# Half of the Winograd weight sums and most left factors made ahead and kept in DRAM, with 35 seven-product quads instead of 26, in an fp32 attention + SSM layer

## The chip, the cores and the metric

One core of a Trainium2 chip runs the kernel. The metric is the device time of one execution in microseconds, as the median of several runs. The engines named below are TensorE (PE, matmuls, with its weight loads shown as PEld), VectorE (DVE), ScalarE (ACT), GpSimd (POOL) and SyncE (SP), whose queue issues nearly all DMAs.

## The reference, cut to what matters

One layer on 256 rows of 2048 values, all in float32. A wide projection feeds an attention half (16 heads of 128) and a state-space half (SSM: 8 groups, 64 heads of 64, state 128, chunks of 128); two sigmoid gates weigh their branches.

```python
hn = rms_norm(x, norm_w)
proj = hn @ w_in            # q, k, v, z_a, z_s, xbc, dt, g_a, g_s
...                         # o_a: attention, times silu(z_a)
...                         # y: conv + SSD scan, times silu(z_s), rms_norm
merged = sigmoid(g_a) * (o_a @ w_attn_branch) + sigmoid(g_s) * (y @ w_ssm_branch)
x = x + merged @ w_out      # then a last rms_norm
```

## The kernel before, in words

**Weights.** The host packs all weights (`lay_weights`, L107) into `wall`, 480 units of 128 x 1024 float32 (512 KB each), in the order in which `weight_plan` (L56) lists the products. A unit passes through one pipeline. `load` (L207) issues its DMA on SP's queue into one of `W_BUFS` = 4 buffers with the tag "w". `unit` (L213) has ACT copy it, rounded, into h (L222) and DVE compute the rest l = w - h (L223), each into one of `H_BUFS` = 4 buffers. The activations are split in the same way, so XT holds high and low halves side by side, and a float32 product becomes h·xh + h·xl + l·xh on PE. The h and l instructions are issued at a priority raised by `L_AHEAD` = 120.

**Stages, in order of time** (by the profile):
- up to 33 us: the first four blocks and dt.
- 33 to 594 us: the SSM part (L759). Each of 8 groups projects B, C and four pairs xs, zs with `gemm_a` (L256, two units each): a "group" of ten projections, 60.1 us where no gate stands in it. Three of the `gs` gate blocks run before groups 0 and 4 and one after group 7 (`gates` L469 with `gemm_b` L330, eight units each). Around these come `conv` (L623), `make_cb` (L634: a product cbp on PE, then cb on DVE), `decays` (L640: ACT, and gt on DVE), `turn` (L661: eight transposes on PE, xdt on DVE), and `scan` (L679: yp on PE, L687; then y, ssq and the split of y into yT on DVE and ACT).
- 594 to 875 us: products of two 512-column blocks with `gemm_pair` (L369): `ssm` blocks 0 and 2 (y times w_ssm_branch, called w_ssm below), then `v` 0 and 2 and `ga` 2.
- 875 to 1175 us: attention (L905). Each of 16 heads projects q, k and za; `scores` (L863: sps on PE, then the softmax on DVE and ACT), `turn_p` (L886: three transposes ptp on PE) and `mix` (L892: ops on PE, then za and oaT on DVE) of earlier heads stand between them.
- up to 1393 us: gates `ga` 0 and 1, the pair `attn` 0, `attn` 2 and 3 by `gemm_b`, the pairs `out` 0 and 2, and the last norm.

**Pairs and quads.** `gemm_pair` works on two row tiles by two column blocks. A quad is two contraction tiles (q counts them), so 2x2 blocks times 2x2 blocks: 8 block products of three matmuls, 24 matmuls. For the quads listed in `S_QUADS` (L40) it uses the Strassen-Winograd form with seven products, 21 matmuls. This form needs four sums of weight blocks: t13 (L432, two of them in one instruction) and two more (L437, L438), all on DVE, each sum then split into h and l (L425, L426). It needs sums of activation blocks too, the "left factors" sx: `turn_x` (L348 to L366), one 512-column addition, four of 128 columns and the splits. Each left factor is made once just ahead of the pair that uses it first (L820 for y, L842 for x, L903 in `mix` for the attention output, sxt_o, and L968) and stays in SBUF for the second pair. `fold` (L458) adds the seven products together.

**Order.** `after`, `tick` and `run_due` (L239 to L254) are a due list written out by hand: a call of `after(n, f)` has f emitted n ticks later, and each projection or quad is one tick (a gate block four). Y_LAG, CB_LAG, GT_LAG, TURN_LAG and S_LAG (L36) are such lags. From the emitted program, Tile's scheduler fixes one order of instructions for each engine when the program is built; at run time each engine works through its own order and waits on semaphores.

Of the kernel before, what the change touches and what calls it, by code (L numbers as in the profile page):

```python
# [9 lines left out]
F32 = mybir.dt.float32  # L10
F32R = mybir.dt.float32r
# [4 lines left out]
P = 128  # L16
S = 256
# [89 lines left out]
def lay_weights(mats):  # L107
    out = np.empty((N_UNITS, P, UNIT), np.float32)
    for tag, form, src, off, n_kt, w in PLAN:
# [6 lines left out]
        if form == "p":  # L116
# [3 lines left out]
            for q in range(n // 2):  # L120
                f = FIRST[tag] + 2 * q
                if q in S_QUADS[tag]:
                    out[f] = np.concatenate([m[q, 0, :, 0], m[q, 1, :, 1]], axis=1)
                    out[f + 1] = np.concatenate([m[q, 0, :, 1], m[q, 1, :, 0]], axis=1)
                else:
                    out[f : f + 2] = m[q].reshape(2, P, UNIT)
# [46 lines left out]
def hybrid_block(ctx: ExitStack, tc: tile.TileContext, wall, xt, x, pk_d, cst_d, fw_d, out):  # L173
# [31 lines left out]
    on_unit = {}  # L205

# [22 lines left out]
    def split(src, hi, lo, scale=1.0):  # L229
# [3 lines left out]
        else:  # L233
            ve.scalar_tensor_tensor(lo, src, scale, hi.bitcast(F32), ALU.mult, ALU.subtract)

# [112 lines left out]
    def turn_x(pool, bufs, temp, x, spare=0):  # L348


        sx = pool.tile([P, 2, 4 - spare, P], F32R, name=f"sx{now[0]}", tag="sx", bufs=bufs)
# [9 lines left out]
        parts = [(sx[:, 0, n], sx[:, 1, n]) for n in range(4 - spare)]  # L361
        if spare:
            own = x[:, 0, P:S], x[:, 0, S + P :]
            split(s[:, 0], *own)
            parts.insert(0, own)
        split(s[:, spare:], sx[:, 0], sx[:, 1])  # L366
        return parts

    def gemm_pair(tag, x_of, n_kt, sxs, swap, extra={}, close=1):  # L369
# [20 lines left out]
        for q in range(n_q):  # L390
            tick()
            if q in extra:
                extra[q]()
# [20 lines left out]
            for m in (n, n + 1):  # L414
                if m not in loaded:
                    load(m)
            wa, wb = loaded.pop(n), loaded.pop(n + 1)
# [11 lines left out]
            with tc.high_priority(L_AHEAD):  # L429
                t13 = mul.tile([P, UNIT], F32, name=f"t13_{n}", tag="t13", bufs=1)  # L430
                b12 = wb[:, :512].unsqueeze(1).to_broadcast([P, 2, 512])
                ve.tensor_tensor(two(t13), b12, two(wa), ALU.subtract)  # L432
# [3 lines left out]
                part(wb[:, 512:], hc[:, :512], lc[:, :512])  # L436
                ve.tensor_tensor(wb[:, :512], wa[:, 512:], t13[:, :512], ALU.subtract)  # L437
# [8 lines left out]
            for acc, x, h, l, cs, own in (  # L446
                (prods[0], a[0][0], ha, la, lo, True),
                (es[1], sx[3], ha, la, hi, False),
                (es[0], a[0][1], hc, lc, lo, False),
                (prods[1], sx[0], ht, lt, lo, True),  # L450
                (prods[3], sx[1], ht, lt, hi, True),
                (prods[2], sx[2], hu, lu, lo, True),
# [101 lines left out]
    with tc.tile_pool(name="ssm", bufs=2) as sp:  # L554
# [203 lines left out]

        for g in range(GROUPS):  # L759
# [9 lines left out]
            for t in range(max(4 * g, 1), 4 * g + 4):  # L769
# [4 lines left out]
                if t % 4 == 3:  # L774
# [6 lines left out]
                    after(y_lag, lambda a=(g, state): scan(*a), 1)  # L781
                conv(collect(acc, f"x{t}"), t, state["xs"][-1][:, i], f"x{t}")
# [25 lines left out]
    def blocks(t, c):  # L808
        return [t[:, i, (c + j) * 512 : (c + j + 1) * 512] for i in range(2) for j in range(2)]

    def two_kts(t, q):
        return t[:, 2 * q : 2 * q + 2, :]

    with tc.tile_pool(name="xp", bufs=1) as xp:
        sxs = {}
        for c in (0, 2):
            for q in S_QUADS[("ssm", c)]:
                if q not in sxs:
                    temp = xp.tile([P, 4, 512], F32, name=f"sxt_y{q}", tag="tmp", bufs=1)
                    sxs[q] = turn_x(xp, 6, temp, two_kts(yT[q // 8], q % 8), 1)  # L820
            es, prods = gemm_pair(
                ("ssm", c), lambda kt: yT[kt // 16][:, kt % 16, :], 2 * KT, sxs, c == 2,
# [210 lines left out]
```

## Time and profile before

| | before |
|---|---|
| median of 3 runs | 1395.88 us (1394.46 to 1396.6) |
| profiled execution: span | 1392.9 us |
| what the median of the runs has above that span | 3.0 us |
| PE, DVE, ACT, POOL busy | 99%, 78%, 58%, 2% |
| DMA over the span | 272.33 MB, 196 GB/s mean |
| w loads | 480 of 512 KB, 3.8 us from issue to landing (median) |

The profiled execution has no time of its own beside its span; what the runs have above it is what lies around the program. The page's second part cuts the span in 40 equal slices:

```
PE   9999999999999999999999999999999999999997
DVE  6897887776787787798988988766676666487887
ACT  7656676675667586665554555555554544454454
DMA  8766675756566665656666566655555655667564
```

Each digit is the busy share of a slice of 34.8 us in tenths (9 is 90% or more). The groups of instructions by line give engine, output and inputs, count, then busy time, mean ns of one, and the idle time just ahead of them with what ended most of it. A busy time of PE counts from start to modelled end, and consecutive matmuls overlap.

### The profile page before, as it was taken

The numbers are of one execution on the slowest core, as the hardware profiler recorded it, in microseconds if no ns is written. First come the engines' busy times: TensorE is split into PE (matmuls) and PEld (weight loads), VectorE is DVE, ScalarE is ACT, GpSimd is POOL, SyncE is SP. The second block draws the span as 40 slices with busy tenths as digits, with TensorE's granted clock in tenths as the row PEclk, the third lists the DMA queues.
The fourth block names the chain that finished last, engine by engine and source line by source line (L and its number), as shares of the span: only waits on it lengthen the run. The fifth ranks groups of instructions, "written<-read, shape, count | busy, mean of one in ns | idle before, by whom it ended". The sixth has DMA issues, their size and how long they took to land.

```text
span 1392.9 us, 19889 instructions
## 1 busy us (share of the span) xinstructions
PE 1381.8 (99%) x7308; PEld 1176.8 (84%) x7308; DVE 1086.8 (78%) x1622; ACT 811.5 (58%) x1258; POOL 32.1 (2%) x86
## 2 busy tenths in 40 slices
PE   9999999999999999999999999999999999999997
PEld 7888888888888888888888888888888888888885
DVE  6897887776787787798988988766676666487887
ACT  7656676675667586665554555554554544454454
POOL 1300000000000000000000000000000000000010
PEclk9999999999999999999999999999999999999999
DMA  8766675756566665656666566655555655667564
GB/s 328 243 196 185 197 215 163 221 185 204 172 212 174 208 189 180 194 181 211 192 206 202 187 212 191 217 174 174 168 174 174 181 170 176 199 212 250 172 198 136
DMA packets 78210, 272.33 MB, mean 196 GB/s; under 512 B 8800, under 2 KB 9376, under 8 KB 77728
## 3 DMA queue, kind: packets, MB, share of 16 engines
q1 hardware_dynamic: 77392, 269.88, 61.9%
q8 instruction: 57, 0.93, 0.3%
q10 hardware_dynamic: 720, 1.18, 0.2%
q14 instruction: 41, 0.34, 0.1%
HBM read 268.86 MB, written 2.16 MB: 195 GB/s over the span
## 4 chain that ended last, share of the span: by engine, by line
PE 98%; DVE 1%; DMA 0%; issue 0%; ACT 0%; SPq 0%; POOL 0%; POOLq 0%; DVEq 0%
PE ps_zs L265 8%; PE ps_xs L265 8%; PE ps_zs L268 4%; PE ps_za L265 4%; PE ps_k L265 4%; PE ps_q L265 4%; PE ps_xs L268 4%; PE ps_ssm L384 3%; PE ps_ssm L385 3%; PE ps_ssm L386 3%; PE ps_q L268 2%; PE ps_k L268 2%; PE ps_za L268 2%; PE ps_gs L345 2%; PE ps_gs L343 2%; PE ps_gs L344 2%
## 5 line engine op out<-in xcount | busy, mean ns | idle before, releaser
L223 DVE TENSOR_TENSOR l<-w,h 128x1024 fp32r<-128x1024 f32 (+1 forms) x432 | 522.8, 1213 | 231.0 <-ACT h L222 229.3
L222 ACT ACTIVATE h<-w 128x1024 fp32r<-128x1024 f32 (+1 forms) x432 | 452.8, 1051 | 407.6 <-issue 104.5
L265 PE MATMUL ps_zs<-XT,h 128*128 128x512 f32 x496 | 174.6, 394 | 0.0
L265 PE MATMUL ps_xs<-XT,h 128*128 128x512 f32 x496 | 174.0, 393 | 0.0
L268 PE MATMUL ps_zs<-XT,l 128*128 128x256 f32 x496 | 139.2, 281 | 0.0
L268 PE MATMUL ps_xs<-XT,l 128*128 128x256 f32 x496 | 138.9, 280 | 0.0
L265 PEld LDWEIGHTS ps_zs<-XT,h 128*128 128x128 f32 x496 | 93.0, 187 | 21.3
L265 PEld LDWEIGHTS ps_xs<-XT,h 128*128 128x128 f32 x496 | 92.9, 187 | 20.9
L268 PEld LDWEIGHTS ps_zs<-XT,l 128*128 128x128 f32 x496 | 93.5, 188 | 1.2 <-issue 1.2
L268 PEld LDWEIGHTS ps_xs<-XT,l 128*128 128x128 f32 x496 | 93.5, 189 | 0.0
L265 PE MATMUL ps_q<-XT,h 128*128 128x512 f32 x256 | 92.3, 404 | 0.0
L265 PE MATMUL ps_k<-XT,h 128*128 128x512 f32 x256 | 89.8, 395 | 0.0
L265 PE MATMUL ps_za<-XT,h 128*128 128x512 f32 x256 | 89.7, 394 | 0.0
L268 PE MATMUL ps_q<-XT,l 128*128 128x256 f32 x256 | 71.1, 278 | 0.0
L268 PE MATMUL ps_za<-XT,l 128*128 128x256 f32 x256 | 71.0, 278 | 0.0
L268 PE MATMUL ps_k<-XT,l 128*128 128x256 f32 x256 | 71.0, 277 | 0.0
L385 PE MATMUL ps_ssm<-l,yT 128*128 128x512 f32 x168 | 65.3, 390 | 0.0
L386 PE MATMUL ps_ssm<-h,yT 128*128 128x512 f32 x168 | 65.0, 389 | 0.0
L384 PE MATMUL ps_ssm<-h,yT 128*128 128x512 f32 x168 | 57.5, 390 | 0.0
L265 PEld LDWEIGHTS ps_za<-XT,h 128*128 128x128 f32 x256 | 48.0, 188 | 11.3
L265 PEld LDWEIGHTS ps_k<-XT,h 128*128 128x128 f32 x256 | 48.0, 188 | 11.2
L265 PEld LDWEIGHTS ps_q<-XT,h 128*128 128x128 f32 x256 | 48.1, 188 | 10.9
(520 smaller groups left out, 2984.3 us busy)
## 6 DMA issues: line engine op xcount, KB each, us to landing
w<-in_wall SPq DMA_DIRECT2D x480, 512.0 KB, 3.8
acb<-acum_d SPq DMA_DIRECT2D x32, 256.0 KB, 3.6
th_s<-in_x SPq DMA_DIRECT2D x4, 512.0 KB, 6.5
vth<-in_x SPq DMA_DIRECT2D x1, 2048.0 KB, 9.3
early<-in_xt SPq DMA_DIRECT2D x7, 256.0 KB, 6.9
fw<-in_fw SPq DMA_DIRECT2D x1, 1024.0 KB, 5.5
out<-vth SPq DMA_DIRECT2D x4, 256.0 KB, 2.8
out<-vth ACTq DMA_DIRECT2D x4, 256.0 KB, 3.2
```

The lines of the kernel that those rows point to most:

```text
L222: ac.activation(h[:, a:b], w[:, a:b], AF.Copy)
L223: ve.tensor_tensor(l[:, a:b], w[:, a:b], h[:, a:b].bitcast(F32), ALU.subtract)
L265: pe.matmul(acc, h[:, kk, :], m, start=(kt == 0), stop=False)
L268: pe.matmul(acc[:, S:], l[:, kk, :], m[:, :S], start=False, stop=(kt == KT - 1))
L343: pe.matmul(accs[i], xh, h[:, kk], start=(kt == 0), stop=False)
L344: pe.matmul(accs[i], xh, l[:, kk], start=False, stop=False)
L345: pe.matmul(accs[i], xl, h[:, kk], start=False, stop=(kt == KT - 1))
L384: pe.matmul(acc, xh, h, start=start, stop=False)
L385: pe.matmul(acc, xh, l, start=False, stop=False)
L386: pe.matmul(acc, xl, h, start=False, stop=stop)
```

## The change

`S_QUADS` lists 35 quads instead of 26: `ssm` 0 and 2 have eight each (five and six before), `v` 0 three (two before), `v` 2, `ga` 2 and `attn` 0 four each (three before); `out` 0 and 2 keep their two each.

**Weight sums.** For each of the 35 quads, a new function `sum_weights` runs ahead of time: it loads one unit (t) and half of another (tb) into two buffers of the "w" ring, and one tick later DVE subtracts twice (512 columns each), and a tick after that `spill` stores the result, 512 KB, from the buffer to a DRAM tile on SP's queue. 27 of these stand in the SSM part, one per 2.5 ticks from tick 16 on (SUMS_SSM); eight, for `attn` and `out`, stand in attention, one per 4 ticks from tick 6 on (SUMS_ATT). `lay_weights` lays the two units of such a quad out the other way to match.

**Left factors.** `keep_left` makes the four of x and the eight of y during the SSM part, with their temporary in the "w" ring and the result in the "h" ring, and stores them (512 KB for one of x, 384 KB for one of y). `fetch_left` loads them at the pair stages: the y factors three quads ahead of their use, the x factors at the start of the `v` pairs. Those of the attention output are made in `mix` as before, but with the temporary in the "w" ring.

**The quad.** A seven-product quad loads unit n (wa), the kept sum (wt) and half of unit n + 1 (wc), three buffers of the ring instead of two; DVE has one subtraction of 1024 columns left (instead of one of 1024 and two of 512), and four splits as before, in another order. `t13` is gone.

```diff
 S_QUADS = {
-    ("ssm", 0): (5, 7, 9, 11, 13), ("ssm", 2): (3, 5, 7, 9, 11, 13),
-    ("v", 0): (4, 6), ("v", 2): (2, 4, 6), ("ga", 2): (2, 4, 6),
-    ("attn", 0): (2, 4, 6), ("out", 0): (3, 5), ("out", 2): (3, 5),
+    ("ssm", 0): (2, 4, 5, 7, 8, 10, 11, 13), ("ssm", 2): (2, 4, 5, 7, 8, 10, 11, 13),
+    ("v", 0): (2, 4, 6), ("v", 2): (2, 4, 5, 6), ("ga", 2): (2, 4, 5, 6),
+    ("attn", 0): (2, 4, 5, 6), ("out", 0): (3, 5), ("out", 2): (3, 5),
 }
+SX_Y = S_QUADS[("ssm", 0)]
+SX_X = S_QUADS[("v", 2)]
+SUMS_SSM = [(t, q) for t in (("ssm", 0), ("ssm", 2), ("v", 0), ("v", 2), ("ga", 2)) for q in S_QUADS[t]]
+SUMS_ATT = [(t, q) for t in (("attn", 0), ("out", 0), ("out", 2)) for q in S_QUADS[t]]
+SSM_FROM, SSM_EVERY, ATT_FROM, ATT_EVERY = 16, 2.5, 6, 4
...
+    presum, lefts = {}, {}
+    def ring(name):
+        return stream.tile([P, UNIT], F32, name=name, tag="w", bufs=W_BUFS)
+    def spill(kept, key, name, src, n):
+        kept[key] = dram.tile([P, n], F32, name=name, tag=name)
+        nc.sync.dma_start(kept[key], src)
+    def sum_weights(tag, q):
+        n = FIRST[tag] + 2 * q
+        t, b11 = ring(f"t{n}"), ring(f"tb{n}")
+        nc.sync.dma_start(t, wall[n + 1])
+        nc.sync.dma_start(b11[:, :512], wall[n, :, :512])
+        def add():
+            ve.tensor_tensor(t[:, :512], t[:, :512], b11[:, :512], ALU.subtract)
+            ve.tensor_tensor(t[:, 512:], t[:, 512:], t[:, :512], ALU.subtract)
+        after(1, add)
+        after(2, lambda: spill(presum, (tag, q), f"t_{tag[0]}{tag[1]}_{q}", t, UNIT))
...
+    def keep_left(key, x, spare):
+        name = f"{key[0]}{key[1]}"
+        temp = ring(f"sxt_{name}").rearrange("p (n m) -> p n m", n=2)
+        sx = stream.tile([P, UNIT], F32R, name=f"sx_{name}", tag="h", bufs=H_BUFS)
+        n = 2 * (4 - spare) * P
+        turn_x(sx[:, :n].rearrange("p (e n s) -> p e n s", e=2, n=4 - spare), temp, x, spare)
+        after(1, lambda: spill(lefts, key, f"sxd_{name}", sx[:, :n].bitcast(F32), n))
...
+    def fetch_left(pool, bufs, key, x, spare):
+        sx = new_sx(pool, bufs, spare, f"{key[0]}{key[1]}")
+        nc.sync.dma_start(sx.bitcast(F32), lefts[key].rearrange("p (e n s) -> p e n s", e=2, n=4 - spare))
+        return left_parts(sx, x, spare)
...
-            wa, wb = loaded.pop(n), loaded.pop(n + 1)
+            wa, wt, wc = ring(f"w{n}"), ring(f"wt{n}"), ring(f"wc{n}")
+            nc.sync.dma_start(wa, wall[n])
+            nc.sync.dma_start(wt, presum[tag, q])
+            nc.sync.dma_start(wc[:, :512], wall[n + 1, :, 512:])
...
-                t13 = mul.tile([P, UNIT], F32, name=f"t13_{n}", tag="t13", bufs=1)
-                b12 = wb[:, :512].unsqueeze(1).to_broadcast([P, 2, 512])
-                ve.tensor_tensor(two(t13), b12, two(wa), ALU.subtract)
                 ha, la = hl(stream, "a", "hl", H_BUFS)
                 part(wa, ha, la)
                 hc, lc = hl(stream, "c", "hl", H_BUFS)
-                part(wb[:, 512:], hc[:, :512], lc[:, :512])
-                ve.tensor_tensor(wb[:, :512], wa[:, 512:], t13[:, :512], ALU.subtract)
-                ve.tensor_tensor(wb[:, 512:], wb[:, 512:], wb[:, :512], ALU.subtract)
+                part(wc[:, :512], hc[:, :512], lc[:, :512])
+                t2 = wt[:, 512:].unsqueeze(1).to_broadcast([P, 2, 512])
+                ve.tensor_tensor(two(wa), two(wa), t2, ALU.subtract)
                 ht, lt = hl(mul, "t", ("ht", "lt"), 2)
-                part(t13, ht, lt)
+                part(wt, ht, lt)
                 hu, lu = hl(mul, "u", ("ht", "lt"), 2)
-                part(wb, hu, lu)
+                part(wa, hu, lu)
...
+        for n, (tag, q) in enumerate(SUMS_SSM):
+            after(SSM_FROM + n * SSM_EVERY - now[0], lambda a=(tag, q): sum_weights(*a))
+        for n, q in enumerate(SX_X):
+            after(SSM_FROM + 4 + 5 * n - now[0], lambda q=q: keep_left(("x", q), two_kts(XT, q), 0))
...
+                    for q in (2 * g, 2 * g + 1):
+                        if q in SX_Y:
+                            after(
+                                y_lag + 2 + q % 2 * 3,
+                                lambda q=q: keep_left(("y", q), two_kts(yT[q // 8], q % 8), 1),
+                            )
...
-                    sxs[q] = turn_x(xp, 6, temp, two_kts(yT[q // 8], q % 8), 1)
+        def left_y(q):
+            sxs[q] = fetch_left(xp, len(SX_Y), ("y", q), two_kts(yT[q // 8], q % 8), 1)
+        extra = {max(q - 3, 0): [lambda q=q: left_y(q)] for q in SX_Y}
...
-                    sx_of_x[q] = turn_x(xp, 3, temp, two_kts(XT, q))
+            sx_of_x[q] = fetch_left(xp, len(SX_X), ("x", q), two_kts(XT, q), 0)
...
-                temp = mul.tile([P, 2, 512], F32, name=f"sxt_o{q}", tag="t13", bufs=1)
-                sx_of_o[q] = turn_x(xp, 3, temp, two_kts(oaT, q))
+                temp = ring(f"sxt_o{q}").rearrange("p (n m) -> p n m", n=2)
+                sx = new_sx(xp, len(S_QUADS[("attn", 0)]), 0, f"o{q}")
+                sx_of_o[q] = turn_x(sx, temp, two_kts(oaT, q))
+        for n, (tag, q) in enumerate(SUMS_ATT):
+            after(ATT_FROM + n * ATT_EVERY, lambda a=(tag, q): sum_weights(*a))
```

More of the change, by code (lines that the diff above doesn't have):

```diff
@@ L360, in turn_x @@
         ve.tensor_tensor(s[:, 3], a12, s[:, 2], ALU.subtract)
-        parts = [(sx[:, 0, n], sx[:, 1, n]) for n in range(4 - spare)]
         if spare:
-            own = x[:, 0, P:S], x[:, 0, S + P :]
-            split(s[:, 0], *own)
-            parts.insert(0, own)
+            split(s[:, 0], x[:, 0, P:S], x[:, 0, S + P :])
         split(s[:, spare:], sx[:, 0], sx[:, 1])
-        return parts
+        return left_parts(sx, x, spare)
     def gemm_pair(tag, x_of, n_kt, sxs, swap, extra={}, close=1):
@@ L391, in gemm_pair @@
             tick()
-            if q in extra:
-                extra[q]()
+            for f in extra.get(q, ()):
+                f()
             ks = [x_of(2 * q + k) for k in range(2)]
```

47 lines of the change are left out of this document (22 added, 25 removed).

## Prediction, made blind

> **What bounds the kernel now.** I read the page first: busy shares, slices, the chain that ended last.
>
> ```profile
> span 1392.9 us, 19889 instructions
> PE 1381.8 (99%) x7308; PEld 1176.8 (84%) x7308; DVE 1086.8 (78%) x1622; ACT 811.5 (58%) x1258; POOL 32.1 (2%) x86
> PE 98%; DVE 1%; DMA 0%; issue 0%; ACT 0%; SPq 0%; POOL 0%; POOLq 0%; DVEq 0%
> ```
>
> TensorE (PE) is busy for 99% of the span and is 98% of the chain. So nothing else costs time until it makes PE wait, and every matmul removed is worth its pitch. Matmul durations overlap, so the pitch is read from the chain in order of time (start, us, what), in the w_ssm stage:
>
> ```profile
> 665.56 0.91 PE ps_ssm L384 x4
> ```
>
> Four matmuls of 512 columns in 0.91 us: 0.2275 us each. The next question is how busy VectorE (DVE) and the DMAs are, by stage: one group of the SSM part, a stretch of w_ssm, attention.
>
> ```profile
> core 0: us, PE busy (x) PEld busy (x) DVE busy (x) ACT busy (x) POOL busy (x), PEclk, DMA share, GB/s
> 426.70:486.80 60.10, 60.10 (x366) 52.14 (x367) 48.69 (x75) 41.50 (x79) 0.61 (x6) 1.00 0.65 193
> 680.00:760.00 80.00, 80.00 (x355) 66.26 (x354) 70.03 (x78) 43.46 (x47) 0.00 (x0) 1.00 0.66 210
> 875.00:1215.00 340.00, 340.00 (x1919) 296.39 (x1918) 221.14 (x411) 169.04 (x254) 0.00 (x0) 1.00 0.59 179
> ```
>
> DVE has 11.4 us free in an SSM group of 60.1, 10.0 in 80 of w_ssm and 119 in attention. The slack that protects PE is shown by the timelines (start, us) around a scan: first PE, then DVE.
>
> ```profile
> 284.56 2.82 PE L687 MATMUL yp<-gt,xdt 128*64 128x256 f32 x32
> 292.83 0.40 PE L343 MATMUL ps_gs<-h,XT 128*128 128x512 f32 x1
> ```
>
> ```profile
> 287.43 0.87 DVE L697 SCALAR_TENSOR_TENSOR y<-xs,pk,yp 128x256 f32<-128x256 f32 x2 [0.41 <-PE yp L687]
> 288.22 0.48 DVE L629 SCALAR_TENSOR_TENSOR cv_x<-raw_x,cw,cv_x 128x256 f32<-128x256 f32 x1
> 288.62 0.69 DVE L700 TENSOR_TENSOR y<-y,zs 128x512 f32<-128x512 f32 x1
> 289.22 1.00 DVE L629 SCALAR_TENSOR_TENSOR cv_x<-raw_x,cw,cv_x 128x256 f32<-128x256 f32 x2
> ...
> 292.45 1.22 DVE L223 TENSOR_TENSOR l<-w,h 128x1024 fp32r<-128x1024 f32 x1
> 293.58 0.42 DVE L328 SCALAR_TENSOR_TENSOR xs<-th_x,cv_x 128x256 f32<-128x256 f32 x1
> 293.92 0.69 DVE L700 TENSOR_TENSOR y<-y,zs 128x512 f32<-128x512 f32 x1
> ...
> 296.80 1.75 DVE L659 TENSOR_TENSOR gt<-gt,cb 128x1536 f32<-128x1536 f32 x1
> ```
>
> yp ends at 287.38; ten DVE instructions later the l of weight unit 99 is ready (292.45 + 1.22 = 293.67). PE asks for it two gs units after 292.83 (24 x 0.2275 = 5.46): at 298.3. Slack 4.6 us. From start to start a DVE instruction costs 0.40 us at 256 elements (0.34 for some), 0.60 at 512, 1.13 at 1024; consecutive ones overlap by 0.08, so gt (1.75) costs 1.67.
>
> **The change, part by part.**
>
> Matmuls: 26 to 35 quads, three matmuls less in each: 9 x 3 x 0.2275 = **-6.1 us** (the built program has 7,062 matmuls, before 7,089). The trace of before has PE without gaps, so no stall is there to be won.
>
> DVE in a seven-product quad, from the groups by line (the last columns: busy, mean ns):
>
> ```profile
> L432 DVE TENSOR_TENSOR t<-w,w 128x1024 f32<-128x1024 f32 x26 | 31.8, 1225 | 18.6 <-DMA w<-in_wall 18.3
> L437 DVE TENSOR_TENSOR w<-w,t 128x512 f32<-128x512 f32 x26 | 17.8, 686 | 0.0
> ```
>
> L432, L437 and L438 (as L437) go and one 128x1024 instruction comes: 1.2 to 1.4 us less per quad. DVE isn't what ends the pair stages, so this counts 0; nor do the left factors that leave them. Half of each sum is now made earlier, 27 of them in the SSM part: two 128x512 subtractions each (1.2 us), one sum per 2.5 ticks and so four per group (a group has ten projections, a tick each). A left factor, one or two per group, costs about 2.2 us: one 512, five or six of 128, one of 384.
>
> ```profile
> 591.45 0.68 DVE L355 TENSOR_TENSOR sxt_y<-yT 128x512 f32<-128x512 f32 x1
> 592.17 0.29 DVE L357 TENSOR_TENSOR sxt_y<-sxt_y 128x128 f32<-128x128 f32 x1
> 592.38 0.28 DVE L358 TENSOR_TENSOR sxt_y<-sxt_y 128x128 f32<-128x128 f32 x1
> ```
>
> (0.20 from start to start at 128.) A group's DVE goes from 48.7 to 48.7 + 4.8 + 2.2 to 4.4 = 56 to 58 of 60.1 us: full, and no longer able to regain a lead.
>
> What decides is the order. It was fixed when the program was built, and the order of the changed program's instructions on PE and DVE shows places where DVE first takes an instruction that waits for PE, then a row of others, and only then the weight split that PE needs next. No lead helps there, since both sides start from the same PE event. Before, the longest run of other work between two splits is 6 us by these prices; after it is 15. The places:
>
> (1) Unit 67 (SSM group 1). PE: unit 66, cbp, unit 67. DVE: cb (waits for cbp), y x2, sx_x, gt, then l67.
>
> ```profile
> L638 DVE TENSOR_TENSOR cb<-cbp,cst x8: 549/558/558, 113.7 to 530.4; 128x384 f32<-128x384 f32 x8
> ```
>
> 0.5 + 0.8 + 0.6 + 1.67 + 1.22 = 4.8 us, in which PE has one matmul. On to l69 (l67 and l68 at 1.13; y, ssq and two subtractions of a sum at 0.6; eight of 256 elements at 0.34 to 0.40) it is 11.8 against 5.6 us of PE work: **6.2**.
>
> (2) Unit 99. From the end of yp to l99 DVE now has 14 instructions of 256 elements (5.6), seven of 512 (4.2), gt (1.67), five of 128 (1.0), one of 384 (0.5) and l99 (1.22): 14.2 us. PE has 5.45 + 5.46, eight transposes (0.87) and one matmul: 12.0. **2.2**. (3) Unit 167, alike: 14.6 against 11.8. **2.8**.
>
> (4) Units 353, 377, 401 in attention. Before, PE goes from a head's scores (sps) to the next head's q unit. In the changed order it does sps, ops, the first transpose of that same head's p, and then the unit: the whole softmax stands ahead of it, with a left factor (sxt_o) in DVE's queue between its steps, and ScalarE (ACT) has the exponentials ahead of the unit's h.
>
> ```profile
> 1056.49 0.55 DVE L869 SCALAR_TENSOR_TENSOR t<-cst,sps 128x384 f32<-128x384 f32 x1
> 1056.95 0.42 DVE L232 TENSOR_TENSOR oaT<-za,oaT 128x256 fp32r<-128x256 f32 x1
> 1057.29 0.28 DVE L873 TENSOR_REDUCE st<-t 128x1 f32<-128x128 f32 x1
> ...
> 1057.81 0.41 DVE L873 TENSOR_REDUCE st<-t 128x1 f32<-128x256 f32 x1
> 1058.26 0.17 DVE L874 TENSOR_SCALAR st<-st 128x2 f32<-128x2 f32 x1
> ...
> 1061.28 0.17 DVE L882 RECIPROCAL st<-st 128x2 f32<-128x2 f32 x1
> 1061.48 0.55 DVE L884 TENSOR_SCALAR p<-p,st 128x128 f32<-128x128 f32 x2
> ```
>
> t 0.46, oaT and za 0.34 each, reduces 0.19 + 0.45, sxt 0.60, st 0.17: 2.6 us; then oaT, two sxt, the two masks with two more sxt behind the exponentials, reciprocal, scaling: about 2.4; then l at 1.22: 6.2 us. PE meanwhile has ops, a transpose and one matmul, 1.1 us. **5.1 each, 15.3**.
>
> (5) Two tighter spots by the same count, units 139 (18.8 against 17.3) and 39 (11.8 against 11.1): 0 to 2.3, I take 1.5.
>
> Sum of the places: 6.2 + 2.2 + 2.8 + 15.3 + 1.5 = **28.0 us**.
>
> Transfers. A sum reads 768 KB and writes 512; four per group and a left factor of 384 KB bring a group from 193 to about 290 GB/s. The nearest rows are those of a busier stretch (35 to 60 us; the last column is us from issue to landing):
>
> ```profile
> DMA packets 1881, 6.62 MB, mean 265 GB/s; under 512 B 207, under 2 KB 334, under 8 KB 1878
> w<-in_wall SPq DMA_DIRECT2D x10, 512.0 KB, 4.1
> ```
>
> Worse than the rate is the ring: t and tb take two of its four w buffers, t until its store has landed. Three buffers serve five units and a tb per 15 us; a turn is at least 0.4 + 4.1 + 1.06 (ACT h) + 1.22 = 6.8 us, so 6 x 6.8 = 41 of 45. In the pair stages a seven-product quad holds three buffers, and three such quads follow each other in v, ga and attn (4, 5, 6): about 26 buffer-us against 4 x 4.8 = 19, on a lead of some 4 us. SP waits for a sum's last subtraction before its store, with the next units' loads queued behind. I can't price these from rows before: below by 0 (all covered), above by 20 (2 us in each of seven groups, 2 in each of three pair stages). I take **4.5**, near the low end: average supply still exceeds demand, and the stalls above give it time.
>
> Sum against the profiled execution: 1392.9 - 6.1 + 28.0 + 4.5 = 1419.3 us of span; the median of the runs, 1395.88, lies 3.0 above the span: **1422 us**.
>
> **The rivals.**
>
> *Faster (4%).* If the order's runs cost nothing, 1395.9 - 6.1 + 0 to 3 = 1390 to 1393. It needs 22 of the 28 us to be wrong; since the waits start from PE's own events, only DVE instructions far shorter than their rows would do that. For it: DVE gets 1.4 us back per quad and the pair stages lose the left factors. *Within 0.2% (2%)*: the same, in part. (0.2% is about what a measurement of this kernel can tell from no change.)
>
> *Only the attention places bind (15%).* If in the SSM part PE arrives late anyway, so that these stalls fall into one another: 15 - 6 = +9, about 1400 to 1412.
>
> *The buffers bind (14%).* If a w load takes 5.5 instead of 4.1 us, a turn is 8.2 and six of them 49 of 45 us: some 4 us per 15 where DVE doesn't cover it. About half of seven groups: +25 or more: 1440 to 1460.
>
> *The clock drops in the stalls (15%).* PE's last matmul ends before 1384:
>
> ```profile
> 1384.00:1388.00 4.00, 0.00 (x0) 0.00 (x0) 2.90 (x6) 1.45 (x3) 1.51 (x4) 1.00 0.72 262
> 1388.00:1393.00 5.00, 0.00 (x0) 0.00 (x0) 0.19 (x1) 0.00 (x0) 0.00 (x0) 0.60 0.58 211
> ```
>
> The granted clock is whole to 1388 and means 0.60 after: if it falls to half, it fell near 1389, 5 us or more after PE stopped. Stalls of 5 us stand just at that. A slow clock is seen at the start:
>
> ```profile
> 4.66 2.16 PE L313 MATMUL ps_first<-yT,h 128*128 128x512 f32 x4
> ```
>
> Four matmuls in 2.16 us, where 0.91 is the full pace; so some 5 us of work pass before it is whole. If four stalls drop it, and each costs half of 5 us, that is +10: 1432. The Trainium skill, "TensorE: Matmul & The Clock Gate", section "Why this matters for your kernels", warns of PE gaps over about 3 us, after which the clock halves; here it was held for about 5; by that page each of the four stalls would drop it.
>
> That the change doesn't do what it says is out: the matmuls are gone from the program.
>
> **How the numbers follow.** Forecast 50% (1412 to 1432, 1422 likeliest); only attention 15%; buffers 14%; clock 15%; faster 4%; same 2%. From 1404 to 1446 leaves out about the low third of "only attention", two thirds of "buffers" and the last two: 20%. Faster 0.04, within 0.2% 0.02, slower 0.94.
>
> **What would show it.** The page after: PE share down to 97%, DVE in its chain with several per cent. PE idle of 4 to 6 us before units 67, 353, 377 and 401, 2 to 3 before 99 and 167, released by DVE l; PE pitch 0.2275 as before. Wrong would be: idle named by DMA w (buffers), PEclk under 1 between 100 and 1380 us (clock), or no PE idle in attention.

## The result and the profile after

The changed kernel takes 1493.71 us (median of 4 runs, 1491.14 to 1496.95), the one before 1395.17 in the same comparison (4 runs): a ratio of 1.0708 (95% interval 1.0689 to 1.0727), far above the range forecast. The profiled execution has a span of 1489.4 us, 96.5 more than before. From its page, the span, the busy shares and the chain that ended last:

```profile
span 1489.4 us, 20257 instructions
PE 1416.3 (95%) x7281; PEld 1184.5 (80%) x7281; DVE 1132.5 (76%) x1693; ACT 831.4 (56%) x1282; POOL 31.7 (2%) x86
PE 44%; DMA 25%; DVE 18%; ACT 6%; issue 5%; SPq 0%; POOL 0%; ACTq 0%; DVEq 0%; POOLq 0%
```

PE was 98% of the chain and is 44%; 25% is now the DMAs, 18% DVE. Where the time went shows when the first matmul of each stage starts, in the two traces:

| first matmul of | before | after | behind by | added in the stage that ends here |
|---|---|---|---|---|
| the SSM part (first gs gate) | 32.8 | 33.6 | 0.8 | 0.8 |
| w_ssm | 580.7 | 644.3 | 63.6 | SSM part 62.8 |
| attention (first q) | 873.7 | 944.2 | 70.5 | pair stages 6.9, with 24 matmuls (5.5 us) fewer |
| ga gates | 1165.0 | 1255.4 | 90.4 | attention 19.9 |
| out | 1298.2 | 1394.0 | 95.8 | gates and attn 5.4 |

In the table of the experiments below, "SSM part" is the column "behind by" at w_ssm (63.6 here). The windows view gives the same (one row of before, the SSM part; three of after: SSM part, pair stages, attention):

```profile
core 0: us, PE busy (x) PEld busy (x) DVE busy (x) ACT busy (x) POOL busy (x), PEclk, DMA share, GB/s
33.00:580.70 547.70, 547.70 (x3179) 471.13 (x3178) 440.16 (x679) 368.88 (x670) 17.18 (x61) 1.00 0.64 198
```

```profile
33.00:645.00 612.00, 573.52 (x3185) 483.06 (x3184) 498.13 (x816) 379.46 (x692) 17.22 (x61) 0.97 0.74 244
645.00:944.00 299.00, 292.48 (x1262) 233.42 (x1261) 239.75 (x245) 167.43 (x181) 1.61 (x1) 1.00 0.70 232
944.00:1255.00 311.00, 299.52 (x1715) 261.47 (x1713) 206.87 (x410) 147.56 (x230) 0.00 (x0) 0.98 0.60 197
```

In the SSM part PE idles 38 us of 612 and runs at a mean clock of 0.97; by the trace's clock record, its six half-clock stretches there cost some 13 us of work. DVE has 58 us more work there and is still only 81% busy. PE's longest waits (us in total, times, longest), then what ScalarE's h waits for between 100 and 580 us, after and before:

```profile
PE ps_zs L298 <- ACT h L249: 11.4, 5, 5.0
PE ptp L940 <- DVE p L935: 11.0, 3, 3.7
PE ps_zs L301 <- DVE l L250: 5.8, 3, 2.8
PE ps_gs L376 <- ACT h L249: 5.7, 1, 5.7
PE ps_C L298 <- ACT h L249: 5.5, 2, 4.9
```

```profile
ACT h L249 <- DMA w<-in_wall: 117.0, 82, 4.7
```

```profile
ACT h L222 <- DMA w<-in_wall: 3.1, 3, 1.4
```

This is the row that the forecast's sum held at little: the rounded weights h now wait for their loads 117 us, where they waited 3. The waits of PE on `ptp` are the three attention places. The third of them in the timeline of PE, and the granted clock around it in the windows view:

```profile
1251.19 0.38 PE L948 MATMUL ops<-pT,vth 128*128 128x128 f32 x2
1255.24 0.45 PE L940 MATMUL ptp<-cst,p 128*128 128x128 f32 x1 [3.67 <-DVE p L935]
1255.34 1.20 PE L376 MATMUL ps_ga<-h,XT 128*128 128x512 f32 x2
```

```profile
1252.00:1254.00 2.00, 0.00 (x0) 0.00 (x0) 2.00 (x9) 1.37 (x4) 0.00 (x0) 1.00 0.00 0
1254.00:1255.00 1.00, 0.00 (x0) 0.00 (x0) 0.96 (x6) 1.00 (x2) 0.00 (x0) 0.75 0.00 0
1255.00:1256.00 1.00, 0.76 (x3) 0.69 (x4) 1.00 (x3) 1.00 (x2) 0.00 (x0) 0.50 0.00 0
...
1260.00:1261.00 1.00, 1.00 (x3) 0.75 (x3) 0.00 (x0) 1.00 (x1) 0.00 (x0) 0.50 1.09 328
1261.00:1262.00 1.00, 1.00 (x5) 0.85 (x4) 0.91 (x1) 0.17 (x2) 0.00 (x0) 0.84 0.82 250
1262.00:1263.00 1.00, 1.00 (x8) 0.85 (x7) 0.76 (x3) 1.00 (x2) 0.00 (x0) 1.00 0.91 336
```

PE stops at 1251.57. The clock is whole to about 1254.5, then half until about 1261.3, six us beyond PE's return: the stall costs 3.7 us and then some 3 us of slow matmuls, which fall into the next stage. Behind the other two the half clock costs some 2.7 and 1.5 us of work. Stalls and half clock make about 15 of attention's 19.9 us; the rest isn't broken down.

### The profile page after: what moved, and what is told of

Read it like the earlier page. It is cut to its first block, busy times and chain, and to the rows that moved or that the text cites. A ratio compares the mean times of both kernels' runs of the same rounds, so it can differ in the third digit from the quotient of the medians.

```text
span 1489.4 us, 20257 instructions
## 1 busy us (share of the span) xinstructions
PE 1416.3 (95%) x7281; PEld 1184.5 (80%) x7281; DVE 1132.5 (76%) x1693; ACT 831.4 (56%) x1282; POOL 31.7 (2%) x86
## 4 chain that ended last, share of the span: by engine, by line
PE 44%; DMA 25%; DVE 18%; ACT 6%; issue 5%; SPq 0%; POOL 0%; ACTq 0%; DVEq 0%; POOLq 0%
DMA w<-in_wall 14%; DVE l L250 5%; PE ps_q L298 4%; PE ps_k L298 4%; PE ps_za L298 4%; DMA tb<-in_wall 3%; ACT h L249 3%; DMA acb<-acum_d 2%; PE ps_q L301 2%; PE ps_za L301 2%; PE ps_k L301 2%; PE ps_zs L298 2%; PE ps_xs L298 1%; DVE ltt L476 1%; PE ps_gs L377 1%
## 5 line engine op out<-in xcount | busy, mean ns | idle before, releaser
L250 DVE TENSOR_TENSOR l<-w,h 128x1024 fp32r<-128x1024 f32 (+1 forms) x414 | 499.9, 1212 | 215.4 <-ACT h L249 211.4
L249 ACT ACTIVATE h<-w 128x1024 fp32r<-128x1024 f32 (+1 forms) x414 | 433.4, 1050 | 400.6 <-DMA w<-in_wall 218.6
L298 PE MATMUL ps_zs<-XT,h 128*128 128x512 f32 x496 | 180.9, 403 | 11.4 <-ACT h L249 11.4
L301 PE MATMUL ps_zs<-XT,l 128*128 128x256 f32 x496 | 142.2, 287 | 5.9 <-DVE l L250 5.8
L476 DVE TENSOR_TENSOR la<-w,ha 128x1024 fp32r<-128x1024 f32 x35 | 42.8, 1223 | 25.3 <-ACT ha L475 25.0
L298 PEld LDWEIGHTS ps_q<-XT,h 128*128 128x128 f32 x256 | 49.7, 194 | 11.1
L697 ACT ACTIVATE gt<-acb,acT 128x128 f32<-128x128 f32 x128 | 43.8, 390 | 17.7 <-DMA acb<-acum_d 17.7
L475 ACT ACTIVATE ha<-w 128x1024 fp32r<-128x1024 f32 x35 | 37.0, 1058 | 26.8 <-DMA w<-in_wall 19.4
```

The source lines that it names most:

```text
L249: ac.activation(h[:, a:b], w[:, a:b], AF.Copy)
L250: ve.tensor_tensor(l[:, a:b], w[:, a:b], h[:, a:b].bitcast(F32), ALU.subtract)
L298: pe.matmul(acc, h[:, kk, :], m, start=(kt == 0), stop=False)
L301: pe.matmul(acc[:, S:], l[:, kk, :], m[:, :S], start=False, stop=(kt == KT - 1))
L475: ac.activation(h, src, AF.Copy)
L476: ve.tensor_tensor(l, src, h.bitcast(F32), ALU.subtract)
```

## The experiments

Each row is one version; the times are in us. The total is the median of its runs; the parts are read from the one profiled execution, from the starts of the first matmuls as above (pair stages: from w_ssm to the first q; attention: from there to the ga gates, each against before). That execution can lie some us off the median: 6.7 above it in c2_all, 6.0 in e9_acbq and 5.1 in d2_all_one_slot, up to 2.9 below it in others. A difference of a few us between two rows says nothing.

| run | what differs | total | SSM part | pair stages | attention |
|---|---|---|---|---|---|
| after | | 1493.7 | 63.6 | 6.9 | 19.9 |
| e6_att | sxt_o outside the ring | 1475.3 | 68.0 | 7.1 | 1.3 |
| e3_no_sums | left factors only | 1466.3 | 39.1 | 7.4 | 21.5 |
| b1_lefts_no_store | e3, hardly any of them stored | 1466.4 | 33.9 | 8.1 | 20.9 |
| b2_lefts_shift | e3, y factors 3 ticks later | 1435.6 | 8.1 | 8.3 | 20.6 |
| e8_shift | after, y factors 3 ticks later | 1489.6 | 60.3 | 7.5 | 20.7 |
| e4_no_lefts | sums only | 1463.8 | 36.3 | 9.4 | 21.1 |
| a1_no_subtract | e4 without the subtractions | 1468.8 | 38.7 | 8.8 | 21.1 |
| a2_subtract_only | e4, only the subtractions | 1432.6 | 5.0 | 8.7 | 20.1 |
| e2_pool | after, stores on GpSimd's queue | 1501.0 | 75.3 | 6.0 | 20.4 |
| e9_acbq | after, acb on ScalarE's queue | 1495.7 | 73.1 | 8.5 | 19.9 |
| e1_stage | after, sums outside the ring | 1482.0 | 54.3 | 7.5 | 21.4 |
| e11_stage_nolefts | e4, sums outside the ring | 1458.3 | 31.5 | 8.1 | 22.4 |
| c4_ring_pool | e4, sums' DMAs on GpSimd's queue | 1469.6 | 34.0 | 11.7 | 21.2 |
| c1_stage_pool | e11 and c4 | 1451.2 | 18.6 | 7.9 | 20.7 |
| d1_one_slot | e11 with one buffer pair | 1467.8 | 40.5 | 7.5 | 21.9 |
| c2_all | after with e6, e8, e1 and the sums' DMAs on GpSimd's queue | 1439.1 | 36.2 | 9.4 | 1.2 |
| d2_all_one_slot | c2 with one buffer pair | 1446.1 | 41.9 | 8.7 | 1.7 |
| c3_quads30 | before with 30 quads | 1402.4 | 0.6 | 5.0 | 2.3 |

### Attention: the temporary in the ring

```diff
-                temp = ring(f"sxt_o{q}").rearrange("p (n m) -> p n m", n=2)
+                temp = mul.tile([P, UNIT], F32R, name=f"sxt_o{q}", tag="ht", bufs=2).bitcast(F32).rearrange("p (n m) -> p n m", n=2)
```

> The changed kernel with one edit: the temporary of the attention output's left factors (sxt_o) back in a buffer of its own (an idle ht buffer) instead of the w ring. Its built order has PE take the next head's unit before that head's first transpose everywhere, as before the change. Order theory: the three stalls of 3.84 us between ops and ptp go, and with them the half clock behind each (about 2.5 us of work each): 18 to 20 us back between the eighth head and the ga gates, total 1472 to 1478. If the left factors' VectorE work made those stalls, they stay at other places: 1485 to 1495.

1475.29 us, a ratio of 1.0577 (1.0547 to 1.0608). PE has no wait at all in attention: 293.00 us busy of 293. **Shown:** with sxt_o as a tenant of the w ring the scheduler fixed an order in which PE takes a head's first transpose ahead of the next weights, three times (heads 7, 11 and 15, counted from 0); with a buffer of its own the order of PE's matmuls in all 16 heads is as before, and 18.6 of the 19.9 us are gone. The left factors' DVE work is the same in both, so it wasn't the work.

### Sums or left factors

Without sums:

```diff
+SUMS_SSM = []
+SUMS_ATT = []
...
-            nc.sync.dma_start(wt, presum[tag, q])
+            nc.sync.dma_start(wt, wall[n + 1])
```

> The changed kernel without the early sums (a quad loads unit n+1 in place of the kept sum, so the result is not the reference's); the left factors are still made early, and 35 quads stay. Ring, queue and rate theories all put the loss on the sums: the SSM part within 10 us of before, total 1400 to 1425, by how much of the attention stalls stays. VectorE theory with the left factors as half of the added work: SSM part still 20 to 30 us longer, total 1425 to 1445.

Without left factors:

```diff
-        for n, q in enumerate(SX_X):
+        for n, q in enumerate(SX_X[:1]):
...
-                        if q in SX_Y:
+                        if q in ():
...
-        nc.sync.dma_start(sx.bitcast(F32), lefts[key].rearrange("p (e n s) -> p e n s", e=2, n=4 - spare))
+        kept = lefts[("x", SX_X[0])][:, : 2 * (4 - spare) * P]
+        nc.sync.dma_start(sx.bitcast(F32), kept.rearrange("p (e n s) -> p e n s", e=2, n=4 - spare))
```

> The changed kernel with only one of the twelve early left factors made and kept (the pair stages load that one in place of all, so the result is not the reference's); all sums stay. Ring, queue and rate theories: the loss stays, with some 5 to 20 us back, 1470 to 1490. VectorE theory: 2.2 to 4.4 of 7 to 9 us of added work per group gone, a third to a half of 66 us back, 1460 to 1472.

Either half alone costs the SSM part 36 to 39 us. Without sums the time lies above both ranges; without left factors it lies in the range of the VectorE theory, which the subtractions alone refute below. Left factors add hardly any transfers and sums no work on ACT; only DVE gets work from both. They had to be followed apart.

### The left factors

Without their stores:

```diff
-        after(1, lambda: spill(lefts, key, f"sxd_{name}", sx[:, :n].bitcast(F32), n))
+        if key == ("x", SX_X[0]):
+            after(1, lambda: spill(lefts, key, f"sxd_{name}", sx[:, :n].bitcast(F32), n))
```

> As the third experiment (no sums, early left factors; SSM part 39 us longer, 1466 in all) with eleven of the twelve left factors made but not stored (the pair stages load the one that is, so the result is not the reference's). If the store makes the loss (SP stands at it until VectorE has the last part, and an h buffer stays taken until it has landed), 15 us or more come back, 1451 or less. If it is the order (a left factor's splits ahead of three units' h on ScalarE, its sums ahead of l on VectorE), 1458 to 1468.

1466.40 us, where e3 had 1466.34: the stores aren't it. Three ticks later, without sums and in the whole change:

```diff
-                                y_lag + 2 + q % 2 * 3,
+                                y_lag + 5 + q % 2 * 3,
```

> As the third experiment (no sums), with the left factors of y emitted three ticks later. All four big SSM stalls of the third experiment (4 to 7.5 us, each behind the turn's transposes) belong to left factors of even q, which fall into the turn's tick. Collision theory: these go, with the half clock behind them, 20 to 35 us back, 1431 to 1446. Otherwise the stalls reappear behind other units and the total stays, 1456 to 1468.

> The changed kernel with the left factors of y emitted three ticks later, so that those of even q no longer fall into the tick of the next group's turn (the eight transposes). Collision theory (without sums, all four big SSM stalls stood right behind those transposes, where three units' h stand behind the left factor's split in ScalarE's order): the stalls of 5 to 6 us at 328 and 556 us go, with their half clock, 12 to 20 us back, 1474 to 1482. Theory of a full resource (VectorE, ring or rate): the same total, 1488 to 1500.

1435.58 us without sums: 31 of the 39 us are gone. The largest wait of PE between 100 us and the end of the SSM part, in e3_no_sums and then in b2_lefts_shift:

```profile
PE ps_C L298 <- ACT h L249: 15.1, 3, 7.4
```

```profile
PE ps_zs L301 <- DVE l L250: 1.6, 1, 1.6
```

What collides is seen in e3's timelines of PE and of ACT, and in that of ACT around the same turn in b2_lefts_shift:

```profile
240.83 1.03 PE L716 MATMUL xtp<-cst,xs 128*128 128x128 f32 x8
245.81 0.51 PE L298 MATMUL ps_C<-XT,h 128*128 128x512 f32 x1 [3.94 <-ACT h L249]
```

```profile
244.28 0.52 ACT L257 ACTIVATE sx_y<-sxt_y 128x384 fp32r<-128x384 f32 x1 [0.23 <-DVE sxt_y L413]
244.71 2.94 ACT L249 ACTIVATE h<-w 128x1024 fp32r<-128x1024 f32 x3
```

```profile
236.56 1.05 ACT L249 ACTIVATE h<-w 128x1024 fp32r<-128x1024 f32 x1
...
238.73 1.05 ACT L249 ACTIVATE h<-w 128x1024 fp32r<-128x1024 f32 x1
...
243.06 1.04 ACT L249 ACTIVATE h<-w 128x1024 fp32r<-128x1024 f32 x1
```

In e3, ACT's order has the left factor's split (sx_y) ahead of three units' h, which stand in a row behind it; in b2 they stand one by one. The split's own wait is short here (0.23 us, for the last of the left factor's small sums on DVE); what costs is the place of h behind it and behind the work ahead of it. **Shown:** in a tick without the turn's transposes the same work costs 8 us, not 39. Not tested is why the scheduler put h there: the left factor sx has a buffer of the h ring, as sxt_o had one of the w ring, and no run gave it a buffer of its own. In the whole change (1489.64 us, outside the range of the collision theory) the two stalls behind the transposes go too, but only 4 us of the total: the weight loads are late for another reason, the sums.

### The sums: arithmetic or transfers

Without the subtractions:

```diff
         def add():
-            ve.tensor_tensor(t[:, :512], t[:, :512], b11[:, :512], ALU.subtract)
-            ve.tensor_tensor(t[:, 512:], t[:, 512:], t[:, :512], ALU.subtract)
+            pass
```

> As the fourth experiment (sums early, one left factor of twelve made; its SSM part was 36 us longer than before, 1464 in all), and now without the sums' subtractions on VectorE: both loads, the ring buffers and the store stay (the result is not the reference's). If transfers, queue and ring make the sums' loss, the SSM part stays 25 to 36 us longer, 1453 to 1466. If VectorE's order and time make it, it goes to under 10 us, 1428 to 1440.

The subtractions alone:

```diff
-        t, b11 = ring(f"t{n}"), ring(f"tb{n}")
-        nc.sync.dma_start(t, wall[n + 1])
-        nc.sync.dma_start(b11[:, :512], wall[n, :, :512])
+        t, b11 = idle[0].rearrange("p k s -> p (k s)")[:, :1024], idle[0][:, 2]
...
-        after(2, lambda: spill(presum, (tag, q), f"t_{tag[0]}{tag[1]}_{q}", t, UNIT))
```

> The counterpart: the sums' subtractions alone, on a buffer that nothing loads or stores, in the SSM part up to the fifth group's scan; no loads, ring buffers or stores of sums (the result is not the reference's), one left factor of twelve. VectorE theory: at the start of group 4 the run is 15 us or more behind before (20 in the fourth experiment), total 1445 to 1460. Transfers, queue and ring theory: under 5 us there, total 1425 to 1435.

1468.76 us (2 to 3 above the range of the transfers theory) and 1432.59 us. The second version subtracts for 24 of the SSM part's 27 sums; those after the fifth group's scan are left out. ACT's h waiting for w from 100 to 580 us, without the subtractions and then with them alone:

```profile
ACT h L248 <- DMA w<-in_wall: 89.2, 40, 7.1
```

```profile
ACT h L253 <- DMA w<-in_wall: 8.0, 9, 1.9
```

**Shown:** the sums' 36 us come with their transfers (the loads, the stores and the buffers that they hold). The subtractions without them, in groups 1 and 2 more than twice as dense as in the change, cost 5 us. A DVE that is nearly full is no cause by itself: the window of group 1 in a2_subtract_only has DVE busy 55 of 60 us and PE without a gap.

```profile
125.00:185.00 60.00, 60.00 (x357) 51.61 (x356) 55.18 (x87) 43.68 (x90) 0.51 (x5) 1.00 0.62 192
```

### Which part of the transfers' way

In the changed kernel waits of SP are new (33 to 594 us). Two of them: w loads that stand until a sum's store has landed, since it holds a ring buffer (with the rows of t_v and t_ga 57.5 us in all), and stores that stand for DVE:

```profile
SPq L238 <- DMA t_ssm<-t: 29.4, 9, 6.4
...
SPq L218 <- DVE t L229: 14.6, 20, 2.2
```

The stores on another queue, the acb loads on another queue, the sums in buffers of their own (a region free until yT1 takes it; in attention the idle ht and lt):

```diff
-        nc.sync.dma_start(kept[key], src)
+        nc.gpsimd.dma_start(kept[key], src)
```

> The changed kernel with the stores of sums and left factors issued on GpSimd's queue, not SP's; ring, DVE work and bytes stay. Queue theory: the loads behind a store no longer wait for DVE, 30 us or more back, 1465 or less. Ring theory: t is held until its store has landed all the same, under 15 us back, 1478 to 1495. VectorE and rate theories: nothing, 1485 to 1500.

```diff
-            nc.sync.dma_start(acb, acum_d[2 * t : 2 * t + 2, :].partition_broadcast(P))
+            nc.scalar.dma_start(acb, acum_d[2 * t : 2 * t + 2, :].partition_broadcast(P))
```

> The changed kernel with the 32 acb loads of the decays on ScalarE's DMA queue instead of SP's. Queue theory: SP then never stands behind an acb whose single buffer ScalarE still reads (38 us of waits, the longest 10.5), the w loads behind it come earlier, 15 to 35 us back, 1460 to 1480. Ring theory: the loads wait for buffers anyway, under 8 us back, 1486 to 1500.

```diff
-        t, b11 = ring(f"t{n}"), ring(f"tb{n}")
+        t, b11 = stage(n)
...
+                early_stage.append(big.tile([P, 16, UNIT // 2], F32, name="stage", tag="yo1"))
+            k = staged[0] % 5 * 3
+            a = early_stage[0].rearrange("p k s -> p (k s)")
+            return a[:, k * 512 : (k + 2) * 512], a[:, (k + 2) * 512 : (k + 3) * 512]
```

> The changed kernel with t and tb outside the w ring: of the 27 sums of the SSM part those between the first and the fifth group's scan use a spare region (the one that yT1 takes later), the others stay in the ring; the eight sums of attention use the idle ht and lt buffers. Every DMA, its queue and all DVE work stay. Ring theory (two of four w buffers are taken by a sum, so ScalarE's h waits for w: 117 us in the SSM part, before 3): most of the 66 us that the SSM part lost comes back where the staging is used, total 1435 to 1455. Queue theory (SP's one queue holds the stores that wait for DVE, loads stand behind): under 15 us back, 1478 or more. VectorE theory (56 to 58 of 60 us busy per group) and transfer-rate theory (235 to 269 GB/s): nothing back, 1485 to 1500.

> The first and the fourth experiment together: sums staged outside the w ring up to the fifth group's scan and in attention, and only one of twelve early left factors made (the result is not the reference's). With the ring and without left factors the SSM part was 36 us longer than before. Ring theory for the sums: the SSM part up to the fifth group within 5 us of before (22 with the ring), total 1440 to 1448. VectorE or rate theory: as in the fourth, 1458 to 1468.

1500.95, 1495.70, 1481.97 and 1458.30 us: none gives back what its theory asked. In e2 GpSimd stands at a store up to 53 us until DVE has written what it is to store, but each of the 27 sums' stores then goes out 0.4 us behind its subtraction and has landed 6.5 us behind it (median; 5.6 in the changed kernel). So SP is rid of the stores, the ring is held only some 1 us longer per sum, and nothing comes back. In e9 ACT's h still waits 118 us for w; its two runs lie 12 us apart. e1 and e11 brought something new. Taking the sums out of the ring takes most of the wait for w loads away: ACT's h (100 to 600 us) in e4, with the ring, and in e11:

```profile
ACT h L249 <- DMA w<-in_wall: 105.1, 72, 3.4
```

```profile
ACT h L268 <- DMA w<-in_wall: 15.7, 13, 2.3
```

But nothing in the ring held the sums back any more, and the order that the scheduler then fixed draws nearly all of them, 45 of 54 subtractions, into groups 1 and 2 (in e11 a window of group 1, then the whole of group 2; the last two columns are DMA share and GB/s):

```profile
125.00:185.00 60.00, 55.42 (x323) 46.98 (x322) 50.36 (x80) 34.43 (x68) 0.51 (x5) 0.94 1.03 407
178.20:258.60 80.40, 69.90 (x398) 58.16 (x397) 68.99 (x111) 45.74 (x91) 0.51 (x5) 0.92 0.96 351
```

The DMA engines are then full or nearly so, and in these two groups e11 loses 25 of its 31 us; in groups 4 and 5, with one sum left, it loses nothing. But in group 2, which loses 20, no wait of ACT names a DMA. The longest waits of PE and of ACT there are for each other and for DVE:

```profile
PE ps_xs L317 <- ACT h L268: 4.3, 2, 2.3
```

```profile
ACT lo_x L371 <- PE ps_xs L320: 10.8, 2, 6.6
...
ACT xs L768 <- DVE y L767: 5.4, 3, 3.1
ACT th_C L379 <- DVE cv_C L696: 5.4, 1, 5.4
```

So full DMA engines stand beside this loss but aren't shown as its cause; DVE works through the drawn-together subtractions there (69 of 80 us busy). So the queue was tried alone, and both together:

```diff
-        nc.sync.dma_start(t, wall[n + 1])
-        nc.sync.dma_start(b11[:, :512], wall[n, :, :512])
+        nc.gpsimd.dma_start(t, wall[n + 1])
+        nc.gpsimd.dma_start(b11[:, :512], wall[n, :, :512])
```

> As the run before it in this list, but with t and tb in the w ring again: only SP's queue is relieved (the result is not the reference's). Queue theory: SSM part under 12 us longer than before, 1428 to 1442. Ring theory: 25 us or more stay there, 1452 to 1470, since a buffer of the ring is freed no earlier than its store, now behind GpSimd's other work, has landed.

> Sums with their subtractions, one left factor of twelve (the result is not the reference's); the sums' buffers outside the w ring up to the fifth group's scan and in attention, and their loads and stores on GpSimd's queue: ring and SP's queue hold what they held before the change, bytes and VectorE work are the change's. If ring and queue together make the sums' loss (36 us in the SSM part), under 10 us are left in the SSM part, total 1428 to 1440. If the transfer rate makes it, it stays: 1455 to 1466.

1469.62 and 1451.18 us: SP's queue alone gives nothing; both together halve the SSM part's loss, and what is left falls in the first groups again. To spread the sums with the ring relieved, one buffer pair instead of five:

```diff
-            k = staged[0] % 5 * 3
+            k = 0
```

> Sums early, one left factor of twelve (the result is not the reference's), the sums' buffers outside the w ring as in the run of the staged sums without left factors, but one such buffer pair instead of five, which spreads the sums over the groups again (with five, 27 sums' worth of loads was drawn into groups 1 and 2, where the DMA engines then stood at 0.8 to 1.0). All their DMAs stay on SP's queue. Ring theory: the SSM part 12 us or less longer than before (36 with the ring), total 1427 to 1442. Queue theory: 25 us or more stay there, 1453 or more. With only SP's queue relieved the SSM part had lost 34.

> The whole change (correct) with every remedy: sxt_o outside the ring, left factors of y three ticks later, the sums of the SSM part up to the fifth group's scan in one buffer pair outside the ring, and their loads and stores on GpSimd's queue. Ring alone (40 us still lost in the SSM part, SP now standing at the one pair 53 us) and queue alone (34) gave nothing. If either of the two holds up the weight loads and both must be relieved, the SSM part loses 8 to 18 us (the subtractions' 5, the shifted left factors' 8, a few sums still in the ring), the pair stages 9, attention none: total 1408 to 1426. If the bytes themselves cost, as when all sums were drawn into two groups, the SSM part stays 25 us or more longer: 1430 or more.

In both traces one of the 23 stores from the pair goes out behind the load of the next sum (at 316 us in d1, 349 in d2), so what is stored there is not the sum; both runs, d2 too against its text, therefore don't compute the reference, and their times are read for the waits alone. 1467.82 and 1446.14 us: the wait only moved, in d1 to SP, which stands before the one pair until DVE has read it, in d2 to DVE, which stands in its own order until a sum's loads, now behind GpSimd's other work, have landed:

```profile
SPq L244 <- DVE stage L247: 52.7, 17, 5.4
```

```profile
DVE stage L247 <- DMA stage<-in_wall: 43.7, 15, 6.3
```

**Left open:** how the 36 us divide between ring, queue and rate. The runs show that relieving the queue alone gives nothing, that relieving the ring takes the wait for w loads from 105 to 16 us but only 5 us of the SSM part's loss, and that each relief tried so far shifted the wait to another engine in whose fixed order it stood. No run relieves the ring and keeps the sums spread out without another wait in its place, so the ring's own share stays open.

### The whole change with the remedies, and the quads alone

> The whole change (correct, nothing left out) with the three remedies: sxt_o outside the ring in attention, left factors of y three ticks later, sums outside the ring up to the fifth group's scan and in attention with their DMAs on GpSimd's queue. If the three causes add up, attention loses nothing, the SSM part 8 to 18 us, the pair stages 7: total 1405 to 1422. If a cause is missed, above 1435. The old kernel's 1395 is not reached in either case, since the pair stages' stalls alone outweigh the 6.1 us of matmuls.

1439.07 us, a ratio of 1.0313 (1.0297 to 1.0329): half of the loss is back, attention's nearly entirely. It lies above the 1435 from which its text called a cause missed: most of the rest is the SSM part, with the sums drawn together as in e11 (32 of 36 us fall in groups 1 and 2), and the pair stages' 9.4 us aren't touched by any remedy. And the added quads without anything early:

```diff
-    ("ssm", 0): (5, 7, 9, 11, 13), ("ssm", 2): (3, 5, 7, 9, 11, 13),
-    ("v", 0): (4, 6), ("v", 2): (2, 4, 6), ("ga", 2): (2, 4, 6),
+    ("ssm", 0): (3, 5, 7, 9, 11, 13), ("ssm", 2): (3, 5, 7, 9, 11, 13),
+    ("v", 0): (2, 4, 6), ("v", 2): (2, 4, 5, 6), ("ga", 2): (2, 4, 5, 6),
```

> The kernel before with 30 seven-product quads instead of 26, as many as its buffers allow (one more in ssm 0, v 0, v 2 and ga 2), sums and left factors made in place as before. 4 x 3 x 0.2275 = 2.7 us fewer of matmuls: 1391.5 to 1393 if its pair stages keep PE fed; 1395 or more if the extra quads starve it as they do in the changed kernel.

1402.38 us, a ratio of 1.0051 (1.0039 to 1.0064): slower with twelve matmuls fewer. In its pair stages PE idles 5.7 us, where before it idled none (the window 594 to 880 us):

```profile
594.00:880.00 286.00, 280.31 (x1223) 227.19 (x1222) 261.70 (x328) 161.11 (x180) 2.62 (x1) 1.00 0.60 193
```

No version beat the kernel before.

## Why the prediction was wrong, point by point

- **What bounds the kernel, and the sign.** Right: PE without gaps, nothing to win but the matmuls, slower.
- **The -6.1 us of matmuls.** The matmuls went, the time didn't: of 5.5 us due in w_ssm, v and ga, the pair stages lost 6.9 instead. ACT's h waits there for w 46.9 us in the changed kernel and 12.0 before (645 to 944, 594 to 873 us):

```profile
ACT h L249 <- DMA w<-in_wall: 46.9, 38, 4.6
```

```profile
ACT h L222 <- DMA w<-in_wall: 12.0, 8, 3.7
```

  Adding quads has a cost of its own, which the sum left out: c3 loses 7.7 us in these stages (5.0, and the 2.7 of matmuls saved) without any early work. Late loads aren't shown as its cause, since ACT's h waits for w 11.1 us there, no more than before; that part stays open.
- **Attention (15.3).** Place and mechanism right, and e6 shows their origin. The stall was 3.67 us, not 5.1: PE waited for p alone, and the matmul of the next unit followed 0.1 us behind the transpose, so the last step of the working, l at 1.22, cost nothing. But the half clock behind the stalls added 1.5 to 3.0 us each. The stage's 19.9 isn't further from the forecast by luck: a stall read 1.4 us too long made up in part for a clock that the sum left out.
- **The places in the SSM part (12.7).** All five named units stall: unit 67 for 7.8 us (5.0 before h, 2.8 before l; 6.2 forecast), 99 for 5.8 (2.2), 167 for 4.9 (2.8), 139 for 3.3 and 39 for 0.8 (1.5 for the two). That is 22 of PE's 38 us; the rest stands at places not named. And PE waits for h more than for l: it is ACT's order, and the loads, that the working left out. At 99 and 167 it is the collision with the turn, worth 31 us when the left factors are alone; the forecast counted the left factors as DVE time only.
- **Transfers (4.5): the step that failed.** "I take 4.5, near the low end: average supply still exceeds demand, and the stalls above give it time." The sums' transfers alone cost 39 us in a1, and h waits 117 us for loads in the changed kernel. The upper bound of 20 was a guess of 2 us per group and stage, with no mechanism that limited it; the average supply was no argument, since loads came late all the same (which of buffers, SP's order and rate made them late stays open). The rival on the buffers named late loads and had 14%, but its premise of 5.5 us per load didn't come: the median was 4.4.
- **The clock.** The forecast read 5 us of hold from the kernel's end and gave a drop 15%. It drops in nine stretches between 100 and 1300 us; summed over the trace's clock record without PE's idle time, they cost 20 us of work, twice what that rival allowed.

## What to carry to other kernels

Work that is moved off the critical engine brings its DMAs, its buffers and its place in every in-order engine's program with it; price each of these, above all a ring that the critical loads use, before counting the engine's free time. When buffers change hands, compare the built order of each engine: a temporary in the wrong ring cost 18 us here without any added work. And count the clock: the three stalls of 3.7 us on TensorE cost 1.4 to 1.8 times their length.

## What the runs showed of the hardware

The half-clock stretches last 3.41, 6.83 or 10.24 us: steps of 3.41. In the changed kernel they begin at 152.00, 223.67, 329.49 us and so on, whole multiples of 3.413 us apart (21 and 31 steps), so when the drop comes after PE stops depends on where the stall falls (after 2.9 us at the stall shown above, 2.2 and 4.1 at the two of the same length before it); stalls of 2.7 and 2.9 us already caused one, and in a1_no_subtract one of 2.2 us did. The Trainium skill, "TensorE: Matmul & The Clock Gate", section "What's actually happening", states a free-running window of 3413 ns; this trace agrees. The prediction's 5 us of hold was one sample of that grid.
